# Layout of a gate scatter in PSUM, and which engine makes its operands and the lower parts of expert weights

## The chip, the cores and the metric

The kernel runs on one core of one Trainium2 chip. A core has TensorE (matrix products into PSUM), VectorE, ScalarE and GpSimd (element-wise work), SyncE (which issues most transfers) and 16 DMA engines. In the profile they are PE, DVE, ACT, POOL and SP, and PEld is the loading of weights into TensorE. The metric is device microseconds (us) of one execution, and less is better.

## The reference

Two layers act on 256 latent and 256 context tokens of width 1024. A layer is a modulated norm, one input projection, four token mixers, their gated merge, and then PEER, a retrieval from 16384 single-neuron experts laid out as a 128 by 128 grid. Only PEER matters here:

```python
def peer(x, wq, keys, u_tab, v_tab):
    q = (x @ wq).reshape(t, PEER_HEADS, 2, PEER_DK // 2)
    s = jnp.einsum('thpd,hpnd->thpn', q, keys)
    sv, si = lax.top_k(s, PEER_TOPK)                 # 16 best rows and 16 best columns of the grid
    cand = sv[:, :, 0, :, None] + sv[:, :, 1, None, :]
    best, pos = lax.top_k(cand, PEER_TOPK)           # 16 best experts per head, 8 heads
    eidx, g = ..., jax.nn.softmax(best, axis=-1)
    act = jax.nn.gelu(jnp.einsum('tkd,td->tk', u_tab[eidx], x))
    return jnp.einsum('tk,tkd->td', g * act, v_tab[eidx])
```

## The kernel before

The first layer routes 512 tokens and the last one 256. The experts of the first 128 tokens of layer 0 are gathered row by row; for all other tokens (three tiles of 128 in layer 0, two in the last layer) the kernel sweeps over all experts. For the sweep it needs, for every token, a dense 128 by 128 map of gates, G[i, j], which is zero but for the chosen experts.

**The scatter** (`scatter`, from line 1449) builds that map on TensorE: for one token, the product of one-hot rows (`ohA`, 128 slots by 128 rows i) and gated one-hot columns (`ohC`, 128 slots by 128 columns j). A tile is 32 steps `q` of four tokens. `hot` (L1468) makes `ohA` or `ohB` for eight tokens in one VectorE comparison, so there are 16 of each per tile. `gated` (L1482, L1484) multiplies four tokens of `ohB` by the gate `gT` and writes `ohC`: on ScalarE as four instructions, one for each token, or as one instruction on GpSimd or VectorE. The table `acts_of` and `pools_of` choose by `q % 5`: in layer 0 ScalarE has 2 and 4 and GpSimd 0, 1 and 3; in the last layer ScalarE has 4, GpSimd 0, 1 and 3, VectorE 2. A step then makes eight matmuls of 128 columns (L1505; a gate is two float16 parts, so two for each token). ScalarE copies the result out of PSUM (L1507) into `blk`, which holds 32 tokens and is stored to DRAM.

The matmuls write token after token, 128 values each. `blk` has the token innermost (32 of them), so that copy reads PSUM in order and writes single values 128 bytes apart.

**Beside the scatter** VectorE finds the best keys and experts of other tiles (`lists`, `select`; in `select` a loop over 15 ranks has one L1427 and one L1428 each), and TensorE computes the first products of the sweep for some expert tiles ahead of time (`u_mm`, L386 to L388: 24 matmuls for each expert tile, into `po`). Their weights come in as `wraw`; ScalarE rounds them to `wh` (L1210), and `wl = wraw - wh`, the lower part, is a subtraction on GpSimd or VectorE (L1211, chosen in `split_u`). Layer 0 computes up to 20 expert tiles ahead, the last layer up to 36.

What the order is set by: the code is written as generators that are interleaved by hand (`both`, `fill.step`), and a scheduler then sets the order of each engine's instructions. Buffers limit how far one engine runs ahead: five or six of `ohC`, three or four of `ohA`, three PSUM tiles `at`. Each engine takes its instructions in order.

Of the kernel before, what the change touches and what calls it, by code (L numbers as in the profile page):

```python
# [13 lines left out]
AF = mybir.ActivationFunctionType  # L14
# [5 lines left out]
P = 128  # L20
# [15 lines left out]
# column offsets in the constant block; the part from N_CST on is used for the Hyena filters only  # L36
# [10 lines left out]
# column offsets in the per-layer small block (partition layout); the part from N_SM on as above  # L47
# [4 lines left out]
# the per-layer row block, broadcast over the partitions  # L52
# [3 lines left out]
# pieces of the modulation: all, those of the first norm, and those that are not for the end of a layer only  # L56
# [4 lines left out]
# those that come during a layer's sweep; but for the first norm's, the last layer needs those of the latents only  # L61
# [3 lines left out]
def unit_order():  # L65
    """the order in which pieces of the weights are used: (layer, kind, index)"""
    o = []
    for l in range(DEPTH):
# [9 lines left out]
        # these are used for one half of the tokens after the other  # L78
# [62 lines left out]
def lay_out(i):  # L141
# [10 lines left out]
    def cols(w):  # L152
        """pieces of 128 columns: [partition = row of a block of 128 rows, block, column]"""
        m = w.shape[1] // 128
        return list(w.reshape(KD, P, m, 128).transpose(2, 1, 0, 3).reshape(m, P, 1024))

    def rows(w):
        """pieces of 4 blocks of rows by 256 columns"""
        m = w.shape[1] // 256
        return list(w.reshape(2, 4, P, m, 256).transpose(3, 0, 2, 1, 4).reshape(2 * m, P, 1024))  # L160
# [63 lines left out]
class Filler:  # L224
    """tensor-engine work that is emitted between the steps of latency-bound work"""
# [29 lines left out]
# of the gates, for their float16 parts  # L255
G_SCALE = 2.0 ** 15
# expert tiles whose first product may run ahead of the second, per layer: in buffers of their own, and in all
NE_OWN = (10, 20)
NE = (20, 36)
# the last expert tiles' second products go result by result  # L260
# [3 lines left out]
def body(ctx, tc, I, out, dbg=None):  # L264
# [28 lines left out]
    class Units:  # L293
# [41 lines left out]
        def next(self, kind):  # L335
            assert order[self.n][1] == kind, (order[self.n], kind)
            # stop at the end of a phase: what follows has other users of the buffers
# [42 lines left out]
    # ---------------------------------------------------------------- helpers  # L380
# [3 lines left out]
    def mm3(ps, w, x, first, last):  # L384
        """one k-step of an exact product of (hi, lo) pairs"""
# [4 lines left out]
    def rstd_of(dst, raw, inv, m):  # L390
        """dst = 1 / sqrt(inv raw + eps), the function's value refined by a Newton step; m is scratch"""
# [6 lines left out]
    def rstd_small(dst, raw, inv, m, t):  # L398
        """the same without the table of another function: a first value from the exponent's bits, three Newton steps"""
# [12 lines left out]
    def table_for_rstd():  # L412
        """loads the activation table that the next rstd_of needs, as soon as no other is needed before"""
# [6 lines left out]
    class Rms:  # L420
        """1/rms over the features of tokens t0..t1, the same on all partitions; fed chunk by chunk"""
# [7 lines left out]
        def square(self, k):  # L429
            if self.ring is None:  # L430
                self.sq[k] = self.sqp.tile([P, T], F32, name="n_sq", bufs=3)
            else:
                # in the memory of weights, which is free at this time
# [5 lines left out]
        def sum(self, k):  # L439
            """pairs of chunks are added first"""  # L440
# [16 lines left out]
    def norm_apply(rm, coef, ia, ib, tok=None):  # L457
        """modulated rows, split; tok takes those of the first 128 tokens with the tokens on the partitions"""
# [35 lines left out]
    def coef_of(l, u, s0=0):  # L494
        """coefficients of a norm, once the modulation is there up to unit u"""
# [7 lines left out]
    def adaln_row(l, u, w, crow, junk):  # L503
        """one piece of the modulation, its columns on the partitions, by the vector engine"""
# [7 lines left out]
    def adaln_lat(l, u, w, crow):  # L512
        """the same for the latents only"""
# [5 lines left out]
    # ---------------------------------------------------------------- start  # L519
# [15 lines left out]
    def adaln_first():  # L535
        """shift and scale of the first norm, two pieces of each at a time"""
# [27 lines left out]
    # ---------------------------------------------------------------- layers  # L564
    for l in range(DEPTH):
# [5 lines left out]
        with ExitStack() as ex:  # L571
# [4 lines left out]
            # the second layer's latents come first  # L576
# [1214 lines left out]
```

## Time and profile before

| | |
|---|---|
| timed runs, us | 3177.6, 3180.3, 3173.1; median 3177.6 |
| span of the profiled execution, us (of its time outside the span the profile shows nothing) | 3172.5 |
| PE, DVE, ACT, POOL busy, share of the span | 93%, 75%, 46%, 27% |

TensorE is busy nearly everywhere. The five tiles of the scatter are the longest stretches in which it is not. They are called A to E here and reach from the ScalarE copy that brings in a tile's rows `iT` to the next tile's, C and E to the last copy `g_first` of their layer: A 684.2 to 742.7, B 742.7 to 820.2, C 820.2 to 887.2 (layer 0), D 2373.4 to 2470.4, E 2470.4 to 2537.7 (last layer). C and E are the last tiles of their layers, which the code calls final. A row of the windows gives the length of a stretch and the time for which each engine was busy in it; where an engine is busy for nearly the whole length, the stretch can't be shorter than its work.

### The profile page before, as it was taken

Reading aid. Unit: us, or ns where it says so; the run is one execution under the profiler, and the core shown is the slowest. Engines: PE = TensorE matmul, PEld = TensorE weight load, DVE = VectorE, ACT = ScalarE, POOL = GpSimd, SP = SyncE. Lnnn points to the kernel's source line nnn. Section 1 sums busy time; section 2 is a strip of 40 time slices with the busy share of each in tenths; the row PEclk is TensorE's granted clock in tenths of the full one; section 3 lists DMA queues with packets and bytes.
Section 4 is the critical chain, followed back from the end, with each engine's and each line's share of the span. In section 5 each row is a group of like instructions: output and inputs, shape, how many; then the busy total and the mean of one; then the engine's idle time right before and its main releaser. Section 6 shows DMA issues by size and latency. Waiting matters only on the chain.

```text
span 3172.5 us, 47568 instructions
## 1 busy us (share of the span) xinstructions
PE 2946.5 (93%) x17500; PEld 2586.1 (82%) x17500; DVE 2387.9 (75%) x4801; ACT 1448.1 (46%) x2367; POOL 854.4 (27%) x557
## 2 busy tenths in 40 slices
PE   8999999977889999999999898999987799999998
PEld 6877778876778998888888796789877698889997
DVE  5775877799988777777878798758689877555555
ACT  5544423558843333323333234465447654555544
POOL 1001100355535454555555411000056300000000
PEclk9999999988889999999999999999989899999999
DMA  7232345434379888898888776334544498666663
GB/s 262 71 113 74 123 141 171 160 113 176 144 268 308 303 297 290 294 323 284 291 286 309 274 270 221 85 114 132 192 135 177 167 318 287 210 206 214 208 196 133
DMA packets 262506, 661.44 MB, mean 208 GB/s; under 512 B 21464, under 2 KB 113632, under 8 KB 261760
## 3 DMA queue, kind: packets, MB, share of 16 engines
q1 hardware_dynamic: 221808, 513.35, 48.3%
q0 software_dynamic: 40464, 145.05, 13.1%
q8 instruction: 137, 2.24, 0.3%
q14 instruction: 97, 0.79, 0.1%
HBM read 609.03 MB, written 49.29 MB: 208 GB/s over the span
## 4 chain that ended last, share of the span: by engine, by line
PE 39%; DVE 17%; issue 12%; DMA 11%; POOL 7%; ACT 2%; POOLq 0%; DVEq 0%; ACTq 0%; SPq 0%
PE mm L1637 6%; PE at L1637 6%; DMA grow<-in_V_dram,gix 6%; POOL grow L1273 5%; PE po L388 4%; PE po L386 4%; PE po L387 4%; PE mm L386 4%; PE mm L387 4%; PE mm L388 4%; POOL wl L1211 2%; DVE ohB L1468 2%; DMA grow<-in_UR_dram,gix 2%; DVE ohA L1468 1%; DMA wraw<-in_W_dram 1%
## 5 line engine op out<-in xcount | busy, mean ns | idle before, releaser
L388 PE MATMUL po<-nh,wl 128*128 128x384 f32 (+1 forms) x2048 | 649.3, 317 | 32.7 <-DVE wl L1211 28.3
L386 PE MATMUL po<-nh,wh 128*128 128x384 f32 (+1 forms) x2048 | 649.3, 317 | 13.7 <-ACT ga L1232 7.8
L387 PE MATMUL po<-nl,wh 128*128 128x384 f32 (+1 forms) x2048 | 645.8, 315 | 0.0
L1210 ACT ACTIVATE vh<-vr 128x1024 fp32r<-128x1024 f32 x254 | 269.5, 1061 | 617.6 <-DMA vr<-in_V_dram 493.1
L388 PEld LDWEIGHTS po<-nh,wl 128*128 128x128 f32 x2048 | 398.3, 194 | 40.8 <-DVE wl L1211 34.0
L386 PEld LDWEIGHTS po<-nh,wh 128*128 128x128 f32 x2048 | 398.0, 194 | 25.3 <-ACT ga L1232 9.3
L387 PEld LDWEIGHTS po<-nl,wh 128*128 128x128 f32 x2048 | 398.3, 195 | 7.4
L1211 DVE TENSOR_TENSOR vl<-vr,vh 128x1024 fp32r<-128x1024 f32 x254 | 334.3, 1316 | 84.7 <-ACT vh L1210 84.3
L1210 ACT ACTIVATE wh<-wraw 128x1024 fp32r<-128x1024 f32 x256 | 269.2, 1053 | 212.9 <-PE po L387 171.2
L386 PE MATMUL mm<-nh,wh 128*128 128x256 f32 (+1 forms) x1056 | 347.7, 331 | 10.0 <-ACT nh L482 3.9
L387 PE MATMUL mm<-nl,wh 128*128 128x256 f32 (+1 forms) x1056 | 342.9, 326 | 0.1
L388 PE MATMUL mm<-nh,wl 128*128 128x256 f32 (+1 forms) x1056 | 341.4, 324 | 0.4 <-POOL wl L326 0.4
L325 ACT ACTIVATE wh<-wraw 128x1024 fp32r<-128x1024 f32 x156 | 164.7, 1057 | 299.5 <-PE mm L387 194.8
L1211 DVE TENSOR_TENSOR wl<-wraw,wh 128x1024 fp32r<-128x1024 f32 x158 | 199.7, 1265 | 122.1 <-ACT wh L1210 122.0
L1211 POOL TENSOR_TENSOR wl<-wraw,wh 128x1024 fp32r<-128x1024 f32 x98 | 241.9, 2471 | 157.0 <-ACT wh L1210 155.6
L1637 PE MATMUL mm<-vl,Wh 128*128 128x512 f32 x635 | 251.8, 397 | 12.1 <-DVE vl L1211 11.7
L1637 PE MATMUL mm<-vh,Wh 128*128 128x512 f32 x635 | 249.6, 393 | 6.6 <-ACT vh L1210 6.5
L1637 PE MATMUL at<-vh,Wh 128*128 128x512 f32 x635 | 250.2, 394 | 0.0
L1637 PE MATMUL mm<-vh,Wl 128*128 128x512 f32 x635 | 249.5, 393 | 0.0
L1637 PE MATMUL at<-vh,Wl 128*128 128x512 f32 x635 | 249.3, 393 | 0.0
L1637 PE MATMUL at<-vl,Wh 128*128 128x512 f32 x635 | 249.2, 392 | 0.0
L1280 DVE SCALAR_TENSOR_TENSOR grow<-grow,mtok 128x1024 f32<-128x1024 f32 x128 | 167.2, 1321 | 106.4 <-DMA grow<-in_UR_dram,gix 106.3
(357 smaller groups left out, 6205.6 us busy)
## 6 DMA issues: line engine op xcount, KB each, us to landing
wraw<-in_U_dram SPq DMA_DIRECT2D x256, 512.0 KB
vr<-in_V_dram SPq DMA_DIRECT2D x254, 512.0 KB
wraw<-in_W_dram SPq DMA_DIRECT2D x190, 512.0 KB
gd<-gblk SPq DMA_DIRECT2D x80, 512.0 KB
G<-gd SPq DMA_DIRECT2D x32, 768.0 KB
grow<-in_W_dram SPq DMA_DIRECT2D x48, 512.0 KB
G<-gd SPq DMA_DIRECT2D x32, 512.0 KB
mw<-in_W_dram SPq DMA_DIRECT2D x16, 512.0 KB
```

The costliest lines, as they stand in the source:

```text
L325: act.activation(h, r, AF.Copy)
L386: pe.matmul(ps, w[0], x[0], start=first, stop=False)
L387: pe.matmul(ps, w[0], x[1], start=False, stop=False)
L388: pe.matmul(ps, w[1], x[0], start=False, stop=last)
L1210: act.activation(h, r, AF.Copy)
L1211: return eng.tensor_tensor(lo, r, h.bitcast(F32), op=ALU.subtract)
L1273: pool.indirect_dma_start(out=q[-1], out_offset=None, in_=tab, in_offset=bass.IndirectOffsetOnAxis(ap=gix[:, p, e:e + 1], axis=0))
L1280: dve.scalar_tensor_tensor(g, g, 1.0, mtok, op0=ALU.mult, op1=ALU.mult, accum_out=dot[:, e:e + 1])
L1468: dve.tensor_tensor(o, iota4[:, None].to_broadcast([P, 2, P, 4]), x[:, t:t + 8].rearrange("p (a b) -> p a b", b=4)[:, :, None, :].to_broad ...
L1637: pe.matmul(accs[i][h], w[a][:, i * 128:(i + 1) * 128], v[b][:, h * 512:(h + 1) * 512], start=j == 0 and a + b == 0, stop=j == P - 1 and a ...
```

## The change

Three edits, and the removal of the comments (three lines are added in all, so that lines behind them have numbers one to three higher):

```diff
-            acts_of = (((2, 4), (2, 4)), ((4,), (4,)))
-            pools_of = (((0, 1, 3), (0, 1, 3)), ((0, 1, 3), (0, 1, 3)))
+            acts_of = (0, 1, 2, 4), (2, 4)
...
-                acts, pools = [x[last][final] for x in (acts_of, pools_of)]
+                acts = acts_of[final]
...
-                        (pool if q % 5 in pools else dve).tensor_tensor(C, B.rearrange("p j t -> p t j"),
+                        dve.tensor_tensor(C, B.rearrange("p j t -> p t j"),
...
-                    ps = at_tile()
+                    ps4 = at_tile().rearrange("p (j t) -> p j t", t=4)
...
-                            pe.matmul(ps[:, z * 128:(z + 1) * 128], A[:, :, z], C[:, z, :, h], start=h == 1, stop=h == 0)
+                            pe.matmul(ps4[:, :, z], A[:, :, z], C[:, z, :, h], start=h == 1, stop=h == 0)
...
-                    evac[0] = act.activation(blk[:, :, o:o + 4].rearrange("p j t -> p t j"),
-                                   ps.rearrange("p (t j) -> p t j", j=128), AF.Copy, scale=1.0 / G_SCALE)
+                    evac[0] = act.activation(blk[:, :, o:o + 4], ps4, AF.Copy, scale=1.0 / G_SCALE)
...
-            halves(h, lo, ur.pop(j), pool if j < (own + 4 if last else 20) or (not last and j % 2) else dve)
+            halves(h, lo, ur.pop(j), lo_eng[0] or (pool if not last and j % 2 else dve))
...
+        lo_eng = [pool if last else dve]
...  in routing(), ahead of the first scatter:
+                lo_eng[0] = dve
...  behind routing() and fill.flush():
+            lo_eng[0] = None
```

1. The four tokens of a step lie innermost in PSUM: a matmul writes 128 values that are 16 bytes apart, and the copy reads PSUM in order and writes runs of four values (16 bytes), 128 bytes apart.
2. GpSimd makes no `ohC`. ScalarE makes 26 of the 32 of tiles A, B and D and 12 of C and E, VectorE the others: 104 or 48 instructions on ScalarE and 6 or 20 on VectorE.
3. `wl` moves by stage: on VectorE while a layer's scatter runs, on GpSimd before it in the last layer, and as before in the sweep.

On ScalarE at the start of tile A, this is the order before (`gblk` is the copy out of PSUM, with the shape that it writes; x4 are the four instructions of one `ohC`):

```order
L1459 ACTIVATE jT<-at 128x128
L1210 ACTIVATE wh<-wraw 128x1024
L1232 ACTIVATE ga<-po_7110 128x384
L1482 ACTIVATE ohC<-ohB,gT 128x128 x4
L1507 ACTIVATE gblk<-at 128x4x128
L1482 ACTIVATE ohC<-ohB,gT 128x128 x4
L1507 ACTIVATE gblk<-at 128x4x128
L1482 ACTIVATE ohC<-ohB,gT 128x128 x4
L1507 ACTIVATE gblk<-at 128x4x128 x2
L1482 ACTIVATE ohC<-ohB,gT 128x128 x4
L1507 ACTIVATE gblk<-at 128x4x128 x3
```

And this is the order on ScalarE at the same place now:

```order
L1460 ACTIVATE jT<-at 128x128
L1483 ACTIVATE ohC<-ohB,gT 128x128 x12
L1509 ACTIVATE gblk<-at 128x128x4 x3
L1483 ACTIVATE ohC<-ohB,gT 128x128 x16
L1509 ACTIVATE gblk<-at 128x128x4
L1483 ACTIVATE ohC<-ohB,gT 128x128 x4
L1509 ACTIVATE gblk<-at 128x128x4
L1483 ACTIVATE ohC<-ohB,gT 128x128 x4
L1509 ACTIVATE gblk<-at 128x128x4
L1483 ACTIVATE ohC<-ohB,gT 128x128 x4
```

ScalarE has about twice the `ohC` between two copies, and the shape of the copy has turned.

On VectorE at the start of tile E, after the gates `gT`, this is the order before:

```order
L1461 SCALAR_TENSOR_TENSOR gT<-at,gT 128x128
L1468 TENSOR_TENSOR ohB<-iota_21480,jT 128x1024
L1468 TENSOR_TENSOR ohA<-iota_21480,iT 128x1024
L1484 TENSOR_TENSOR ohC<-ohB,gT 128x512
L1468 TENSOR_TENSOR ohB<-iota_21480,jT 128x1024
L1468 TENSOR_TENSOR ohA<-iota_21480,iT 128x1024
L1468 TENSOR_TENSOR ohB<-iota_21480,jT 128x1024
L1468 TENSOR_TENSOR ohA<-iota_21480,iT 128x1024
L1484 TENSOR_TENSOR ohC<-ohB,gT 128x512
```

And this is the order on VectorE at the same place now:

```order
L1462 SCALAR_TENSOR_TENSOR gT<-at,gT 128x128
L1469 TENSOR_TENSOR ohB<-iota_21564,jT 128x1024
L1485 TENSOR_TENSOR ohC<-ohB,gT 128x512 x2
L1469 TENSOR_TENSOR ohA<-iota_21564,iT 128x1024
L1485 TENSOR_TENSOR ohC<-ohB,gT 128x512
L1469 TENSOR_TENSOR ohB<-iota_21564,jT 128x1024
L1469 TENSOR_TENSOR ohA<-iota_21564,iT 128x1024
L1485 TENSOR_TENSOR ohC<-ohB,gT 128x512
L1469 TENSOR_TENSOR ohB<-iota_21564,jT 128x1024
L1469 TENSOR_TENSOR ohA<-iota_21564,iT 128x1024
L1485 TENSOR_TENSOR ohC<-ohB,gT 128x512
L1211 TENSOR_TENSOR wl<-wraw,wh 128x1024
```

VectorE now makes more than half of the final tile's `ohC`, and lower parts stand between them. On GpSimd all 100 `ohC` are gone, and of 98 lower parts of `u_mm` 63 are left: 54 in layer 0's sweep, as before, and 9 ahead of tile D.

Counted in the order up to each tile's last instruction on the engine: the first products' matmuls on TensorE in A to E were 54, 192, 155, 337, 313 and are 68, 216, 153, 213, 432. The `wl` on VectorE in A to E were 0, 0, 1, 1, 4 and are 5, 7, 5, 11, 11.

## Rows read from the trace of the kernel before

**Rows 1.** The page: the span of the profiled execution.

```profile
span 3172.5 us, 47568 instructions
```

**Rows 2.** Windows of A to E: length, busy us (count) by engine, clock, DMA.

```profile
684.20:742.70 58.50, 44.45 (x352) 38.38 (x352) 56.49 (x152) 51.67 (x95) 27.83 (x22) 0.76 0.35 140
742.70:820.20 77.50, 60.36 (x452) 55.29 (x450) 74.73 (x214) 58.80 (x106) 46.70 (x29) 0.85 0.43 154
820.20:887.20 67.00, 53.79 (x432) 48.42 (x433) 64.23 (x219) 52.83 (x97) 36.14 (x24) 0.85 0.42 157
2373.40:2470.40 97.00, 71.09 (x622) 66.28 (x622) 95.63 (x272) 60.65 (x95) 58.27 (x33) 0.89 0.45 158
2470.40:2537.70 67.30, 54.48 (x522) 51.39 (x522) 52.57 (x52) 52.77 (x84) 28.08 (x20) 0.91 0.49 180
sum 367.30, PE 284.17 PEld 259.76 DVE 343.64 ACT 276.72 POOL 197.02; mean PE 56.83 PEld 51.95 DVE 68.73 ACT 55.34 POOL 39.40
```

**Rows 3.** Groups by line: busy us, mean ns, idle before and its releasers.

```profile
L1505 PE MATMUL at<-ohC,ohA 128*128 128x128 f16 x1280 | 107.8, 239 | 60.9 <-DVE ohA L1468 36.2 <-ACT gblk L1507 15.1 <-POOL ohC L1484 4.2
L1484 POOL TENSOR_TENSOR ohC<-ohB,gT 128x512 f32<-128x512 f16 x100 | 129.8, 1309 | 109.3 <-DVE ohB L1468 52.4 <-PE at L1505 32.6 <-DVE gT L1461 12.0
```

**Rows 4.** Timeline, VectorE then GpSimd: start us, duration us, engine, line, operation.

```profile
762.69 0.67 DVE L1468 TENSOR_TENSOR ohA<-iota,iT 128x1024 f16<-128x1024 f16 x1
763.28 0.08 DVE L1330 MATCH_VALUE_LOAD rep<-sv,mm 128x8 f32 x1
773.55 2.75 DVE L1468 TENSOR_TENSOR ohB<-iota,jT 128x1024 f16<-128x1024 f16 x1
772.90 2.85 POOL L1211 TENSOR_TENSOR wl<-wraw,wh 128x1024 fp32r<-128x1024 f32 x1
```

**Rows 5.** Windows of lines 1468 (in E, summed), 1428 and 1427 (summed).

```profile
2470.40:2537.70 67.30, 30.38 (x32) 0.91 0.49 180
sum 367.30, DVE 170.19; mean DVE 34.04
sum 367.30, DVE 27.40; mean DVE 5.48
sum 367.30, DVE 19.87; mean DVE 3.97
```

**Rows 6.** Single lines on VectorE: shortest/median/longest ns, first and last start.

```profile
L1428 DVE COPY_PREDICATED ij<-sf,sif x90: 421/446/2590, 669.4 to 2468.9; 128x256 f32<-128x256 uint16 x90
L1427 DVE TENSOR_SCALAR sf<-ab x90: 199/226/2340, 669.0 to 2468.6; 128x256 f16<-128x256 f16 x90
L1484 DVE TENSOR_TENSOR ohC<-ohB,gT x12: 678/1541/2758, 2380.1 to 2511.2; 128x512 f32<-128x512 f16 x12
L1211 DVE TENSOR_TENSOR wl<-wraw,wh x158: 1205/1225/3404, 874.2 to 3089.8; 128x1024 fp32r<-128x1024 f32 x158
```

**Rows 7.** ScalarE: two rows of the timeline, two groups by shape.

```profile
775.25 2.48 ACT L1482 ACTIVATE ohC<-ohB,gT 128x128 f32<-128x128 f16 x8
762.88 2.89 ACT L1507 ACTIVATE gblk<-at 128x512 f32<-128x512 f32 x3
L1507 ACT ACTIVATE gblk<-at 128x512 f32<-128x512 f32 x160 | 160.3, 1113 | 19.4 <-PE at L1505 18.7
L937 ACT ACTIVATE k<-at 128x512 f32<-128x512 f32 x48 | 28.6, 596 | 31.8 <-PE at L382 31.4 <-ACT wb L331 0.2
```

**Rows 8.** TensorE: four rows of the timeline; the windows of the keys.

```profile
775.51 0.67 PE L1505 MATMUL at<-ohC,ohA 128*128 128x128 f16 x8 [0.55 <-ACT gblk L1507]
775.98 0.42 PE L386 MATMUL po<-nh,wh 128*128 128x384 f32 x1
769.44 0.33 PE L388 MATMUL po<-nh,wl 128*128 128x384 f32 x1
769.61 0.33 PE L386 MATMUL po<-nh,wh 128*128 128x384 f32 x1
sum 367.30, PE 14.93 PEld 12.52 POOL 0.00; mean PE 2.99 PEld 2.50 POOL 0.00
```

More of the change, by code (lines that the diff above doesn't have):

```diff
@@ L1483, in gated @@
                     else:
-                        (pool if q % 5 in pools else dve).tensor_tensor(C, B.rearrange("p j t -> p t j"),
-                                                                    gT[:, t:t + 4][:, :, None].to_broadcast([P, 4, P]), op=ALU.mult)
+                        dve.tensor_tensor(C, B.rearrange("p j t -> p t j"),
+                                          gT[:, t:t + 4][:, :, None].to_broadcast([P, 4, P]), op=ALU.mult)
                     Cs[q] = C.rearrange("p t j -> p (t j)").bitcast(F16).rearrange("p (t j s) -> p t j s", t=4, s=2)
```

## Prediction

> **What bounds the kernel now.** I read the windows by slice first. TensorE is busy nearly everywhere, so only a stretch in which it idles or runs at the low clock can give time back, and the five tiles of the scatter, A to E, are the longest. They take 367.3 us of a span of 3172.5 [rows 1, 2]; TensorE is busy for 284.2 of that, so it idles 83, and its granted clock is 0.76 to 0.91, which means that part of the time it runs at the lower of its two levels (1.2 instead of 2.4 GHz). Then I looked for the engine without gaps: in A to D VectorE is busy 291.1 of 300.0 us (97%). In E no engine fills the stretch: TensorE has 54, VectorE and ScalarE 53 each of 67 [rows 2]. The groups by line confirm it: the scatter's matmuls wait longest for `ohA` from VectorE, then for the copy out of PSUM by ScalarE [rows 3]. So A to D are as long as VectorE's work there.
>
> Last I looked at single instructions on VectorE. The same one-hot takes 0.67 us, and the next instruction starts 0.59 after it, or 2.75 us; the slow one began while GpSimd was in a subtraction of 2.85 us, and both ended about together [rows 4]. Two-input work on VectorE and GpSimd holds each other up. The change takes GpSimd out of the scatter.
>
> **VectorE, part by part, in A to D.**
> One-hots: 170.2 us in all, 30.4 of them in E, so 139.8 for 128 in A to D [rows 5]. At 0.59 they are 76: **-64**.
> The loop over ranks in `select` (three passes of 15, all in A, B and D) takes 27.4 + 19.9 = 47.3 us; at its medians, 0.446 + 0.226, 45 pairs are 30 [rows 5, 6]: **-17**. Other two-input instructions of `select` gain too; I count nothing for them.
> `ohC`: 38 instead of 6. The shortest of before is 0.678, their median 1.54 [rows 6]. 38 at 0.68 less 6 at 1.54: **+17**. If they stayed at 1.54 with GpSimd idle, it would be +49; I take the shortest, because the long ones stood beside GpSimd.
> `wl`: 28 instead of 2 at 1.225 [rows 6]: **+32**. They had been hidden on GpSimd; now they stand in the queue ahead of the one-hots that TensorE waits for.
> Sum: 291 - 64 - 17 + 17 + 32 = 259. At the same 97% that is 267 us instead of 300, 11% less: B's 77.5 becomes 69, C's 67 becomes 60, D's 97 becomes 86.
>
> **ScalarE.** An `ohC` is four instructions, 0.31 each in a row (2.48 for eight), and a copy 0.96 (2.89 for three) [rows 7]. A, B and D get 14, 14 and 20 `ohC` more, 56, 56 and 80 instructions: +17, +17, +25 us. Against this stands the copy: written 128 bytes apart value by value it takes 1.113, while a copy of the same size that reads PSUM and writes in order takes 0.596 [rows 7]. No row shows runs of four values. The bounds are 0.596 and 1.113; I take 0.60, the nearer case in kind, since neighbours come together again. In proportion a copy then costs 0.52 in a row instead of 0.96, 14 us less per tile. ScalarE's work becomes about 55, 62, 38 and 71 in A to D, below or level with VectorE's. So ScalarE isn't the bound, but in B and D it is close, and it needs the cheaper copy for that.
> The Trainium skill (SBUF — State Buffer, Specifications (TRN2)) gives SBUF lines of 16 bytes and a penalty for each access that crosses to a new one. A run of four float32 is one such line, so by this rule the copy costs the contiguous 0.60; without it, 1.11, the third rival below.
>
> **TensorE.** Eight scatter matmuls take 0.47 (775.51 to 775.98), 59 ns each; a first product of 384 columns in layer 0 takes 0.17 (769.44 to 769.61), and one of 256 columns in the last layer by its columns 0.116 [rows 8]. With the counts of the new order a tile has 256 x 0.059 = 15 us of scatter, and first products of 68 x 0.174 = 12, 216: 38, 153: 27 (layer 0), 213 x 0.116 = 25 and 432: 50. The products with the keys, 15 us in all, go to A to D. So TensorE needs 31, 56, 46, 43 and 65 us at the full clock.
> To this comes what a matmul costs whose 128 results lie 16 bytes apart. The trace shows no such matmul. Lower bound: nothing. Upper bound: ScalarE's rate when it writes apart, 0.96 us for 512 values, 1.9 ns each, 243 ns for 128, so +185 ns per matmul. Between the two I take the ratio by which ScalarE's copy is slower apart than in order, 1.113 / 0.596 = 1.87: 110 instead of 59 ns, +52 ns, 13.3 us per tile. That makes 44, 69, 59, 56 and 78.
> In A, C and D this lies beside VectorE's 259; in B it is level with it. In E it decides: 78 instead of 67.3, also because 432 first products stand there instead of 313 and VectorE, which loses 11 us on one-hots, is not needed for so long.
>
> **Sum.** A to D 267 (-33), E 78 (+11): **-22 us**. First products that move between tiles, and lists that moved ahead, are inside these numbers. GpSimd's lower parts in layer 0 that ran ahead of A go to VectorE too, 3 us by the order, but the selection that stands there also stops meeting GpSimd; I count 0 for the two. The sweep behind, where TensorE is the bound and `wl` goes as before, is taken as unchanged. The profiled span of 3172.5 becomes 3150, and the median of the runs shown, 5 above that span, 3177.6 - 22 = **3155**. Late next is TensorE in E and B, and ScalarE in D.
>
> **The rivals.**
> *TensorE pays more for the stride* (slower). Place: the eight matmuls of every step; price up to +185 ns each. Then the tiles need on TensorE 31, 56, 46, 43, 65 with 47 us more each: 78, 103, 93, 90, 112, in all 476 instead of 367: **3287**. It decides from about +100 ns per matmul, where 241 + 1280 x 0.1 = 369: eight matmuls would then take 1.27 us instead of 0.47. For it: nothing else in the trace writes PSUM apart, and ScalarE shows that writing apart is not free; TensorE already has the longest work in E. Against it: TensorE idles 83 us there and runs partly at the low clock, so the first part of the price is covered.
> The Trainium skill (PSUM — Partial Sum Buffer, Specifications (TRN2)) speaks for this one: PSUM lines are 8 bytes, and any access pattern that isn't contiguous "slows matmuls significantly"; it gives no figure. By it the rival's chance can't be small, and a zero price is unlikely.
> *The stride costs TensorE nothing.* E falls to 65, A to D stay with VectorE: 332 instead of 367, -35, and the uncounted instructions of `select` may add 2 or 3: **3140**. For it: a matmul of 384 columns goes at the same rate per column as one of 128 [rows 8], so PSUM writing isn't seen to limit anything now.
> *The copy stays at 1.11* (the edit of the layout does nothing for ScalarE). Then ScalarE has 69, 76, 53 and 85 in A to D. It sets A and B, VectorE sets C (60) and D (86), and with E at 78 that is 369, no change: **3179**. For it: the runs are still 128 bytes apart. Against it: three of four values follow their neighbour.
>
> **Chances and range.** Moderate stride price as summed: 0.45. No price: 0.22. More than +100 ns: 0.21. Copy unchanged: 0.12. The first case by itself spans 3130 to 3175, because the share of 97% may drop when VectorE, ScalarE and TensorE come so near to each other. To hold 8 in 10 the range goes down to 3115 (no price, and more gain in `select`), and up to 3220 (+130 ns per matmul: 241 + 166 = 407 instead of 367, and a few us more). What a measurement of this kernel can tell from no change is about 0.2%, 6 us. Faster: 0.45 x 0.85 + 0.22 x 0.97 + 0.12 x 0.3 = 0.63; slower: 0.21 x 0.95 + 0.45 x 0.05 + 0.12 x 0.25 = 0.25; the same: the rest, 0.12.
>
> **What the profile would show.** Right: one-hots of 0.67 us nearly everywhere in the five tiles; copies near 0.60; eight scatter matmuls in 0.8 to 1.0 us; A to D together near 267 with VectorE busy over 94%; E longer than 67. Eight matmuls in 0.47 would be the second rival, in 1.3 or more the first; copies of 1.1 the third. The prediction falls altogether if one-hots stay slow without GpSimd, or if the time comes or goes outside the five tiles.

## The result, and where the time went

The kernel after takes 3129.9 us in the median (3123.5 to 3141.8, four runs); the kernel before, on the same chip, takes 3176.3 (3173.1 to 3180.3). The ratio is 0.987, 95% interval 0.984 to 0.989. In the profiled executions the span falls from 3172.5 to 3125.5, by 47.0 us. Lines 1468, 1484, 1505 and 1507 of before are 1469, 1485, 1507 and 1509 now.

The windows of the five tiles of after, bounded as in [rows 2]; the columns are length, busy us (count) of PE, PEld, DVE, ACT and POOL, TensorE's granted clock, DMA share and GB/s:

```profile
679.90:742.50 62.60, 52.42 (x359) 45.59 (x360) 57.00 (x221) 55.39 (x152) 0.00 (x0) 0.94 0.38 142
742.50:817.80 75.30, 72.25 (x494) 67.17 (x493) 69.44 (x285) 62.33 (x162) 0.00 (x0) 0.98 0.45 163
817.80:875.20 57.40, 53.29 (x386) 50.57 (x385) 54.34 (x162) 44.01 (x103) 2.39 (x1) 0.97 0.59 219
2338.40:2416.60 78.20, 66.04 (x497) 61.48 (x497) 72.26 (x275) 62.54 (x165) 0.00 (x0) 0.92 0.47 170
2416.60:2488.20 71.60, 71.60 (x618) 70.89 (x618) 51.20 (x70) 52.99 (x117) 0.00 (x0) 1.00 0.59 205
sum 345.10, PE 315.61 PEld 295.69 DVE 304.25 ACT 277.26 POOL 2.39; mean PE 63.12 PEld 59.14 DVE 60.85 ACT 55.45 POOL 0.48
```

Against [rows 2] A has grown by 4.1 us and E by 4.3; B, C and D are shorter by 2.2, 9.6 and 18.8. That is -22.2 in the tiles. GpSimd has left them (197.0 us busy, now 2.4), TensorE's work is done at a higher granted clock (A 0.94 instead of 0.76), and in E it is busy from end to end: 71.60 of 71.60.

The groups of after by line (busy us, mean ns, and idle time of the engine before them with what ended it); the matmuls and the copy answer to [rows 3, 7], the one-hots to [rows 5]:

```profile
L1507 PE MATMUL at<-ohC,ohA 128*128 128x128 f16 x1280 | 163.1, 313 | 15.8 <-ACT gblk L1509 13.1 <-DVE sf L1429 0.7 <-DVE ohC L1485 0.6
...
L1509 ACT ACTIVATE gblk<-at 128x512 f32<-128x512 f32 x160 | 92.6, 598 | 17.9 <-PE at L1507 17.4
...
L1469 DVE TENSOR_TENSOR ohA<-iota,iT 128x1024 f16<-128x1024 f16 x80 | 54.3, 681 | 10.2 <-PE at L1507 10.2
L1469 DVE TENSOR_TENSOR ohB<-iota,jT 128x1024 f16<-128x1024 f16 x80 | 54.3, 679 | 3.6 <-ACT ohC L1483 3.6
```

The one-hots take 0.68 us wherever they stand (shortest 0.662, longest 0.696). In before, the windows give 170.2 us for them, in after 105.8. A copy takes 0.598 instead of 1.113. TensorE's idle time before scatter matmuls is 15.8 us instead of 60.9, and what ends it is the copy.

TensorE in E (start, duration, line, operation). The sixteen scatter matmuls of two steps stand between first products, so the start of the next product shows where they end:

```profile
2443.40 0.28 PE L388 MATMUL po<-nh,wl 128*128 128x256 f32 x1
2443.52 1.94 PE L1507 MATMUL at<-ohC,ohA 128*128 128x128 f16 x16
2445.21 0.36 PE L386 MATMUL po<-nh,wh 128*128 128x256 f32 x1
2445.41 0.28 PE L387 MATMUL po<-nl,wh 128*128 128x256 f32 x1
```

Sixteen matmuls reach from 2443.52 to 2445.21, 106 ns each, where [rows 8] has 59. The granted clock is 1.00 in E now.

The other 24.8 us of the 47.0 lie outside the tiles: A starts 4.3 us earlier, between C's end and D's start there are 23.0 less (1486.2, now 1463.2), and behind E there are 2.5 more. Three pairs of rows tell of the middle part. First the indices that start layer 0's gather (the row-by-row fetch of the experts of the first 128 tokens), which `select` of tile 0 makes at its end (count, shortest/median/longest ns, first and last start), in before and in after:

```profile
L1438 DVE SCALAR_TENSOR_TENSOR gix<-ij x1: 282/282/282, 916.4 to 916.4; 128x128 int32<-128x128 f32 x1
```

```profile
L1440 DVE SCALAR_TENSOR_TENSOR gix<-ij x1: 282/282/282, 894.7 to 894.7; 128x128 int32<-128x128 f32 x1
```

They come 21.7 us earlier while C's end comes 12.0 earlier. Then the start of D, TensorE's transposition of D's `ij`, with the idle time before it and its releaser in brackets, in before and in after:

```profile
2372.49 0.90 PE L382 MATMUL at<-kc,ij 128*128 128x128 f32 x3 [10.19 <-DVE ij L1428]
```

```profile
2337.47 0.90 PE L382 MATMUL at<-kc,ij 128*128 128x128 f32 x3 [5.25 <-DVE ij L1430]
```

TensorE waits 4.9 us less there for the loop over ranks. Last comes the middle of layer 0's sweep, as a window from 1180 to 1780 in before and in after:

```profile
1180.00:1780.00 600.00, 570.09 (x2818) 513.31 (x2817) 468.27 (x466) 186.85 (x268) 318.92 (x206) 0.99 0.86 295
```

```profile
1180.00:1780.00 600.00, 572.78 (x2860) 516.47 (x2859) 473.88 (x464) 191.66 (x275) 327.51 (x208) 0.99 0.87 298
```

The code is the same there, yet TensorE executes 2860 instructions in these 600 us instead of 2818. Whether that belongs to the change is asked below.

### The profile page after: what moved, and what is told of

Its sections match the earlier page's. It is cut to its first block, busy times and chain, and to the rows that moved or that the text cites. A ratio compares the mean times of both kernels' runs of the same rounds, so it can differ in the third digit from the quotient of the medians.

```text
span 3125.5 us, 47587 instructions
## 1 busy us (share of the span) xinstructions
PE 2969.2 (95%) x17500; PEld 2615.0 (84%) x17500; DVE 2330.2 (75%) x4882; ACT 1447.3 (46%) x2583; POOL 640.8 (21%) x422
## 4 chain that ended last, share of the span: by engine, by line
PE 51%; DVE 12%; DMA 10%; issue 8%; POOL 5%; ACT 2%; POOLq 0%; DVEq 0%; ACTq 0%; SPq 0%
PE mm L1640 8%; PE at L1640 8%; PE po L388 6%; PE po L386 6%; PE po L387 6%; DMA grow<-in_V_dram,gix 5%; PE mm L386 4%; PE mm L387 4%; PE mm L388 4%; POOL grow L1275 3%; PE at L1507 2%; POOL wl L1211 2%; DMA vr<-in_V_dram 1%; DMA wraw<-in_W_dram 1%; DMA grow<-in_UR_dram,gix 1%
## 5 line engine op out<-in xcount | busy, mean ns | idle before, releaser
L387 PE MATMUL po<-nl,wh 128*128 128x384 f32 (+1 forms) x2048 | 639.0, 312 | 0.0
L1211 DVE TENSOR_TENSOR wl<-wraw,wh 128x1024 fp32r<-128x1024 f32 x193 | 239.7, 1243 | 128.6 <-ACT wh L1210 128.4
L386 PEld LDWEIGHTS mm<-nh,wh 128*128 128x128 f32 x1056 | 203.6, 194 | 35.4 <-issue 6.0
```

The costliest lines, as they stand in the source:

```text
L386: pe.matmul(ps, w[0], x[0], start=first, stop=False)
L387: pe.matmul(ps, w[0], x[1], start=False, stop=False)
L1211: return eng.tensor_tensor(lo, r, h.bitcast(F32), op=ALU.subtract)
```

## The experiments

All times are medians, and ratios are to the kernel before with a 95% interval. In the table tiles are bounded by TensorE alone, so that all kernels are measured alike: from the first transposition of a tile's `ij` to that of the next, C and E to the last scatter matmul. The stretches come from one profiled execution of each kernel, the last column is the median of all. `gix` to D reaches from the indices to D's start, and "rows" from the issue of the first fetched row of layer 0's gather to that of the last. By these bounds before has 364.2 us in the tiles and after 343.8.

| kernel | A | B | C | D | E | sum | C's end to D | `gix` to D | rows | us |
|---|---|---|---|---|---|---|---|---|---|---|
| before | 55.7 | 80.3 | 65.7 | 97.0 | 65.5 | 364.2 | 1487.5 | 1456 | 882 | 3176 |
| after | 58.4 | 77.8 | 57.7 | 77.8 | 72.1 | 343.8 | 1464.6 | 1443 | 876 | 3130 |
| e1 layout undone | 63.3 | 82.6 | 61.4 | 87.4 | 66.4 | 361.2 | 1476.4 | 1453 | 884 | 3159 |
| e2 turned by the copy | 56.2 | 72.4 | 56.6 | 77.1 | 60.4 | 322.6 | 1480.9 | 1457 | 890 | 3125 |
| e3 pairs | 58.3 | 76.2 | 57.7 | 78.7 | 72.0 | 342.9 | 1468.2 | 1446 | 881 | 3129 |
| e4 GpSimd in vain | 69.4 | 83.9 | 73.0 | 87.2 | 87.1 | 400.7 | 1475.1 | 1453 | 886 | 3189 |
| e5 lower parts undone | 56.8 | 72.4 | 60.0 | 76.4 | 81.5 | 347.0 | 1487.5 | 1471 | 899 | 3154 |
| e6 columns back | 74.8 | 65.9 | 61.9 | 90.6 | 65.6 | 358.6 | 1473.2 | 1458 | 889 | 3155 |
| e7 layout alone | 55.8 | 79.1 | 68.0 | 96.9 | 67.2 | 367.0 | 1491.1 | 1461 | 890 | 3173 |
| e8 lists late | 56.9 | 79.5 | 63.6 | 75.6 | 72.6 | 348.1 | 1492.4 | 1440 | 874 | 3155 |
| e9 after again | 58.5 | 76.2 | 56.3 | 78.6 | 72.1 | 341.6 | 1472.7 | 1451 | 886 | 3134 |
| e10 turned, balanced | 54.7 | 76.0 | 57.1 | 76.6 | 68.9 | 333.4 | 1468.1 | 1453 | 885 | 3127 |
| e11 four rows | 57.1 | 81.4 | 55.7 | 78.5 | 72.0 | 344.8 | 1407.6 | 1383 | 818 | 3070 |
| e12 e10 and e11 | 55.4 | 77.8 | 57.3 | 75.9 | 70.2 | 336.6 | 1408.2 | 1395 | 829 | 3061 |

**e1: the layout undone.**

```diff
-                    ps4 = at_tile().rearrange("p (j t) -> p j t", t=4)
+                    ps = at_tile()
-                            pe.matmul(ps4[:, :, z], ...
+                            pe.matmul(ps[:, z * 128:(z + 1) * 128], ...
-                    evac[0] = act.activation(blk[:, :, o:o + 4], ps4, ...
+                    evac[0] = act.activation(blk[:, :, o:o + 4].rearrange("p j t -> p t j"), ps.rearrange("p (t j) -> p t j", j=128), ...
```

> The kernel after, with PSUM laid out token by token again (matmuls write in order, the copy writes apart); engines and lower parts as after. Theory: the layout was needed because ScalarE got the columns. Copies go from 0.60 back to 1.11 us, +14 us of ScalarE per tile: 69, 76, 58 and 77 us of work in A to D where after has stretches of 62.6, 75.3, 57.4 and 78.2, so A to D grow by about 20; matmuls fall from 106 to 59 ns, and E loses 2 to 4. Sum about +18: 3148, 0.991 of before. Rival: ScalarE has room for the old copy, and the stride only costs TensorE time: A to D unchanged, E from 71.6 to 60: 3118 to 3120.

3158.6 us, 0.994 (0.9915 to 0.9963). The groups of its matmuls and its copy:

```profile
L1507 PE MATMUL at<-ohC,ohA 128*128 128x128 f16 x1280 | 121.1, 249 | 58.1 <-ACT gblk L1509 46.8 <-DVE ohA L1469 3.3 <-DVE ohC L1485 1.9
L1509 ACT ACTIVATE gblk<-at 128x512 f32<-128x512 f32 x160 | 164.8, 1107 | 3.3 <-PE at L1507 3.1
```

The copy takes 1.107 us again, and TensorE waits 46.8 us for it. A to D grow by 23, E falls by 5.7: together 17.4, as the theory has it. The whole is 10 us above the forecast, because another 12 lie between C's end and D's start. The rival falls: with the columns on ScalarE, the kernel needs the cheaper copy.

**e2: the copy turns.** PSUM as in e1, and the copy reads apart what it writes in runs:

```diff
+                    evac[0] = act.activation(blk[:, :, o:o + 4], ps.rearrange("p (t j) -> p j t", j=128), ...
```

> The kernel after, with PSUM laid out token by token (matmuls write in order), and the copy itself turns: it reads PSUM 512 bytes apart and writes runs of four values. Theory: the old copy's price, 1.11 instead of 0.60 us, is that of writing value by value to places 128 bytes apart; reading PSUM apart costs little. Copies 0.60 to 0.65, matmuls 59 ns: E, bound by TensorE at 71.6, falls to 62 to 64 (ScalarE and VectorE have 53 and 51), A to D stay or lose 5: 3115 to 3122, 0.982 of before. Rival: ScalarE pays for walking apart on either side: copies 1.0 to 1.1, and the time is that of the layout undone, about 3148.

3124.9 us, 0.983 (0.980 to 0.986). That is 3 us above the forecast, and the difference from after is within the intervals. The groups, and sixteen scatter matmuls in E with the first product behind them:

```profile
L1507 PE MATMUL at<-ohC,ohA 128*128 128x128 f16 x1280 | 112.5, 242 | 28.7 <-ACT gblk L1509 25.1 <-DVE ohC L1485 1.7 <-DVE sf L1429 1.0
L1509 ACT ACTIVATE gblk<-at 128x512 f32<-128x512 f32 x160 | 90.0, 600 | 8.6 <-PE at L1507 8.1
...
2441.76 1.13 PE L1507 MATMUL at<-ohC,ohA 128*128 128x128 f16 x16
2442.70 0.36 PE L386 MATMUL po<-nh,wh 128*128 128x256 f32 x1
```

The copy takes 0.600 us though it reads PSUM 512 bytes apart, and a matmul takes 59 ns again (16 in 0.94 us). So the price of 1.113 in before lay on the side that writes single values, and TensorE need not pay for the layout. E falls from 72.1 to 60.4 and the tiles by 21. Of this only about 5 us arrive in the whole: D starts 7 us later than in after, though C ends 9 earlier. The table shows where the rest goes: from `gix` to D's start it takes 1457 us instead of 1443, and that is the gather, 890 us from the first row to the last instead of 876. In A and D TensorE's granted clock is 0.71 and 0.77, where after has 0.92 in both: with the shorter matmuls TensorE stands idle for longer there (26.9 us of the two stretches, in after 20.5).

**e3: pairs.** Two tokens innermost in PSUM:

```diff
+                    ps2 = at_tile().rearrange("p (a j t) -> p a j t", a=2, t=2)
+                            pe.matmul(ps2[:, z // 2, :, z % 2], A[:, :, z], ...
+                    evac[0] = act.activation(blk[:, :, o:o + 4].rearrange("p j (a t) -> p j a t", t=2), ps2.rearrange("p a j t -> p j a t"), ...
```

> The kernel after, with two tokens innermost in PSUM instead of four: a matmul's results lie 8 bytes apart instead of 16, the copy reads pairs and still writes runs of four. Theory: a matmul pays because each value falls into a line of its own; at 8 bytes this holds as at 16, so matmuls stay at 106 ns and the time at 3130 (E 71.6). Rival: the price grows with the distance: 59 ns at 4 bytes, 106 at 16, so 75 at 8, E falls by 6 to 66: 3123. Copies 0.60 if reading in pairs is free; at 1.1 A to D grow by 20.

3128.8 us, 0.985 (0.982 to 0.989). Scatter matmuls in E and the first product behind them:

```profile
2442.63 1.94 PE L1507 MATMUL at<-ohC,ohA 128*128 128x128 f16 x16
2444.33 0.36 PE L386 MATMUL po<-nh,wh 128*128 128x256 f32 x1
```

Sixteen in 1.70 us, 106 ns each: results 8 bytes apart cost what they cost 16 bytes apart, and the rival falls. The Trainium skill (PSUM — Partial Sum Buffer, Specifications (TRN2)) has lines of 8 bytes and says that matmuls are slowed significantly by an access that isn't contiguous; the 106 ns of TensorE's writing agree with it. In e2 ScalarE's reading shows no such price.

**e4: GpSimd in vain.** After, and for three of five steps

```diff
+                        X = gp.tile([P, 4, P], F16, name="ohX", bufs=1)
+                        pool.tensor_tensor(X, iota4.rearrange("p j t -> p t j"), gT[:, t:t + 4]..., op=ALU.mult)
```

> The kernel after, and beside it GpSimd multiplies a constant table by the gates for three of five steps, as it did for the columns before, into a tile that nobody reads (written as float16). Nobody waits for it. Theory: two-input work on GpSimd holds up that on VectorE, whatever waits for it: the one-hots go from 0.66 to a mean of 0.9 to 1.1 us, A to E grow by 35 to 60 us: 3165 to 3190. Rival: before lost its time because VectorE and TensorE queued behind results that GpSimd delivered late: one-hots stay at 0.66 to 0.70, and the time at 3130, within 5.

3189.3 us, 1.004 (1.002 to 1.006): slower than before. One-hots, and GpSimd's instruction:

```profile
L1469 DVE TENSOR_TENSOR ohA<-iota,iT 128x1024 f16<-128x1024 f16 x80 | 75.9, 952 | 2.9 <-PE at L1511 2.8
L1469 DVE TENSOR_TENSOR ohB<-iota,jT 128x1024 f16<-128x1024 f16 x80 | 74.3, 930 | 1.1 <-ACT ohC L1483 1.1
...
L1489 POOL TENSOR_TENSOR ohX<-iota,gT 128x512 f16<-128x512 f16 x100 | 140.0, 1400 | 213.0 <-DVE gT L1462 205.6
```

Nobody waits for `ohX`, yet the one-hots take 0.94 instead of 0.68 us and the tiles 400.7 instead of 343.8. VectorE is busy 373 us in them instead of 303. The queue behind late results, the rival, explains nothing of this: it is the two engines side by side. VectorE's work grows by half a microsecond for each that GpSimd works. The Trainium skill (SBUF — State Buffer, Who interferes with whom) says that a VectorE instruction with two inputs in SBUF contends with a GpSimd instruction that reads SBUF, for a port pair that is locked and not shared; the one-hots' 0.94 us fit that.

**e5: lower parts undone.**

```diff
-            halves(h, lo, ur.pop(j), lo_eng[0] or (pool if not last and j % 2 else dve))
+            halves(h, lo, ur.pop(j), pool if j < (own + 4 if last else 20) or (not last and j % 2) else dve)
```

> The kernel after, with the choice of the engine for the lower parts (wl) as in before: GpSimd while the scatter runs, layout and columns as after. Theory: GpSimd's two-input work costs VectorE about as much as it saves. From the run with GpSimd in vain: 142 us of GpSimd lengthened VectorE's work by 70, half a microsecond for each. 28 lower parts of 2.6 us are 73 us of GpSimd, so +36 on VectorE, and 28 x 1.2 = 34 go from it: A to E within 10 of after's 344, and 3130 to 3145 in all, since TensorE waits longer for each lower part. Rival: the move of the lower parts was a cost that the rest of the change paid for: VectorE loses 34 us of work in A to D, which is its bound, and the time falls to about 3105.

3153.9 us, 0.994 (0.991 to 0.997). In the tiles the theory holds, 347.0 us and so within 10 of 344: those of layer 0 are 4.7 us shorter than in after, E is 9.4 longer. But the whole costs more than the theory's upper end, because from `gix` to D's start it takes 28 more. The rival falls. Of the 28, 23 lie between the first and the last row of the gather, 899 us, the longest of all; what makes it the longest, I couldn't show.

**e6: the columns back on GpSimd.**

```diff
-            acts_of = (0, 1, 2, 4), (2, 4)
+            acts_of, pools_of = ((2, 4), (4,))[last], (0, 1, 3)
-                        dve.tensor_tensor(C, ...
+                        (pool if q % 5 in pools else dve).tensor_tensor(C, ...
```

> The kernel after, with the columns (ohC) divided as in before: GpSimd does steps 0, 1 and 3 of five; layout and lower parts as after. Theory: 100 columns of 1.3 us on GpSimd lengthen VectorE's work by 65 us and take 40 us of columns from it: +25, and E, where no VectorE time is to spare once its one-hots slow down, grows too. A to E about 365 instead of 344, 3145 to 3160. Rival: with the lower parts off GpSimd and the cheaper copies, the columns are no harm there, and VectorE and ScalarE have less to do: 3120 or lower.

3154.7 us, 0.995 (0.993 to 0.997), as the theory has it. The tiles take 358.6, and the scatter matmuls wait for one-hots again, 20.6 us:

```profile
L1507 PE MATMUL at<-ohC,ohA 128*128 128x128 f16 x1280 | 159.9, 318 | 27.2 <-DVE ohA L1469 20.6 <-POOL ohC L1485 3.4 <-ACT gblk L1509 2.9
```

**e7: the layout alone**, on the kernel before; three lines of the change:

```diff
+                    ps4 = at_tile().rearrange("p (j t) -> p j t", t=4)
+                            pe.matmul(ps4[:, :, z], ...
+                    evac[0] = act.activation(blk[:, :, o:o + 4], ps4, ...
```

> The kernel before with the new layout in PSUM alone: matmuls at 106 instead of 59 ns, copies at 0.60 instead of 1.11 us, engines as in before. Theory: in A to D VectorE held up by GpSimd sets the end, so the copies bring nothing or little there; in E TensorE gets 12 us more: 0 to +10, 3176 to 3186. Rival: the copy was a bound in itself (TensorE waited 15 us for it): 3155 to 3165, and the layout would be half of what the change brings.

3172.6 us, 1.000 (0.9991 to 1.0013); the profiled execution, at 3182.6, is the longest of ten. The copy falls to 0.592 us, the matmuls rise to 106 ns, and the tiles stay (367.0 by 364.2). In A to D VectorE is busy for 286.0 of 299.8 us, so both are hidden there, and E grows by 1.7. By itself this edit is worth nothing, and the rival falls.

**e8: lists late.**

```diff
-                    next(others, 0)
+                    if z >= 10:
+                        next(others, 0)
```

> The kernel after, with the lists of tile 0 begun in step 10 instead of step 0 of tile C: VectorE does the same work, but more of it behind C's last column. Theory: what starts layer 0's sweep is the end of VectorE's work (scatter and selection of tile 0 together), not the end of the scatter: C ends some 5 to 10 us earlier, the selection ends at the same time within 3 (its last index at 895), and the whole stays at 3130 within 5. Rival: the sweep follows C's end, so what C gains the whole gains: 3120 to 3125.

First products have by then overwritten the queries that these lists read, so tile 0's selection has other values here, in the same amount, and other rows are fetched. 3154.6 us, 0.995 (0.993 to 0.997). Both theories missed. C doesn't end earlier, and the selection ends 33 us later than in after:

```profile
L1440 DVE SCALAR_TENSOR_TENSOR gix<-ij x1: 278/278/278, 927.5 to 927.5; 128x128 int32<-128x128 f32 x1
```

The order has moved more than I meant: the lists had stood in B, where VectorE has gaps now (61 busy of 79.5 us), and stand behind C. What it shows is a link: `gix` 33 us later, C's end 2 later, the gather's last row 31 later (1801.9 instead of 1770.9), D's start 30 later. The sweep's second products begin at 893.1, as in after (891.7). So D doesn't follow the end of the scatter or the beginning of the sweep, but the gather, which starts at the end of the selection.

**e9: after again**, unchanged.

> The kernel after once more, unchanged. Between C's end and D's start its profile has 23 us less than before, and part of it lies in the middle of layer 0's sweep, which the change doesn't touch: from 1180 to 1780 us TensorE executes 2860 instructions in after, 2818 in before, and 2773 to 2817 in the eight other kernels. Theory: this is the spread of an execution. The new profile has 2780 to 2830 there, and C's end to D's start takes 1470 to 1485 instead of 1464.6; the median stays within 0.987 +- 0.002 of before. Rival: it belongs to the program: 2850 to 2870 and 1462 to 1468 again.

3134.3 us, 0.9875 (0.986 to 0.989).

```profile
1180.00:1780.00 600.00, 567.37 (x2806) 511.03 (x2805) 469.84 (x453) 188.27 (x269) 320.36 (x206) 0.98 0.86 293
```

2806 instead of 2860, and C's end to D takes 1472.7, as the theory has it. The window of 600 us is not a property of the change, and two profiles of one kernel differ by 8 us between C and D. Most of the 23 stays all the same. In both profiles `gix` comes 21.8 us after C's end where before has 31.4, and D starts 564 to 567 us after the gather's last row where before has 574: some 17 us in all. Between them lies the gather, with 876 and 886 us around before's 882.

**e10: turned, balanced.** On e2:

```diff
-            acts_of = (0, 1, 2, 4), (2, 4)
+            acts_of = ((0, 1, 2, 4), (0, 1, 2, 3, 4))[last], ((0, 2, 4), (2, 4))[last]
```

> The kernel in which the copy turns, and the columns divided anew: ScalarE makes all of D's (four of five before) and three of five of C's (two before). Theory: C and D are bound by VectorE (55 of 56.6 and 73 of 77.1 us, ScalarE 44 and 61); six columns of 0.68 less in each are -4 each, ScalarE then has 52 and 69: 3117 instead of 3125, 0.981 of before. Rival: other waits end last there by now, or the gain of the tiles is lost in the sweep behind: 3125.

3126.6 us, 0.985 (0.983 to 0.986). The rival holds: C has 57.1, D 76.6, as in e2. The five tiles are even 11 us longer than in e2, by B and E above all; but C's end to D is 13 shorter, of which 9 because `gix` comes 15 us after C's end instead of 24, and the whole is the same. VectorE has 66 of D's 76.6 us now, so it isn't the bound there any more. TensorE's longest wait in D is the one for copies, 15.5 us (10.9 in e2):

```profile
PE at L1507 <- ACT gblk L1509: 15.5, 17, 2.6
```

Whether this wait or the granted clock, 0.73 there, now sets D's end, no run separates.

**e11: four rows.** On after; in layer 0 the gathered rows have four buffers, and a row is fetched three ahead (and what makes room for it):

```diff
-            rows = lambda: up.tile([P, D], F32, name="grow", bufs=3)
+            rows = lambda: up.tile([P, D], F32, name="grow", bufs=4 - l)
-                for e in range(P + 2):
+                for e in range(P + 3):
...
-                    if e < 2:
+                    if e < 3:
                         continue
-                    e -= 2
+                    e -= 3
```

> The kernel after with four buffers instead of three for the gathered rows of layer 0, so that a row is fetched three ahead instead of two (to make room, four ohC instead of five in layer 0 and a lead of 4 instead of 5 steps; a junk tile in float16). Theory: in the sweep of layer 0 VectorE waits 125 us in the 600 between 1180 and 1780 for gathered rows; these waits stand ahead of wl and vl, for which TensorE then waits 27 us, and this sets how fast the sweep goes and why its time differs from kernel to kernel. One row more ahead: VectorE waits under 60, TensorE's idle time there falls by 15 to 25 us, and the whole to 3095 to 3115. Rival: rows come as fast as DMA brings them (its share is 0.87): the waits stay above 110, and so do 3130.

3069.8 us, 0.968 (0.9665 to 0.969): 60 us below after, where 15 to 35 were expected. VectorE's longest waits in the window from 1180 to 1780 (us in total, times, longest), in before and in after:

```profile
DVE gacc L1284 <- DMA grow<-in_V_dram,gix: 78.2, 35, 4.5
DVE grow L1280 <- DMA grow<-in_UR_dram,gix: 47.0, 26, 3.7
DVE gacc L1282 <- DMA grow<-in_V_dram,gix: 4.8, 1, 4.8
```

```profile
DVE gacc L1286 <- DMA grow<-in_V_dram,gix: 80.8, 38, 4.3
DVE grow L1282 <- DMA grow<-in_UR_dram,gix: 36.9, 19, 4.2
DVE gacc L1284 <- DMA grow<-in_V_dram,gix: 7.1, 1, 7.1
```

And in e11, with its window:

```profile
DVE grow L1282 <- DMA grow<-in_UR_dram,gix: 8.2, 6, 2.5
DVE gacc L1286 <- DMA grow<-in_V_dram,gix: 4.5, 4, 2.2
```

```profile
1180.00:1780.00 600.00, 599.93 (x3043) 547.69 (x3042) 510.62 (x519) 214.84 (x291) 322.75 (x202) 1.00 0.90 312
```

The waits for gathered rows fall from 125 us to 13, TensorE has no gap left, and it executes 3043 instructions instead of 2860. A row lands 6.1 to 6.7 us after its issue, by the median of the transfers in after:

```profile
grow<-in_UR_dram,gix POOLq DMA_INDIRECT x128, 6.7
grow<-in_V_dram,gix POOLq DMA_INDIRECT x128, 6.1
```

An expert tile is 42 matmuls (24 of the first product, 18 of the second), so 2860 are 68 tiles, 8.8 us each, and each uses two or three rows. With three buffers a row can't be fetched before the row three ahead of it has been used, and VectorE stands still until it lands, with `wl` and `vl` behind it in its queue. So the gather set the pace of layer 0's sweep in before, which has the same waits (130 us), and in after, and TensorE, 95% busy there, only looked like the bound.

The buffers are not all of it. In after, GpSimd and VectorE around one such wait:

```profile
1415.16 2.41 POOL L1211 TENSOR_TENSOR wl<-wraw,wh 128x1024 fp32r<-128x1024 f32 x1
1417.72 1.09 POOL L1275 DMA_INDIRECT grow<-in_V_dram,gix  x1 [0.16 <-issue]
1411.73 2.60 DVE L1286 SCALAR_TENSOR_TENSOR gacc<-grow,gdot,gacc 128x1024 f32<-128x1024 f32 x2
1425.94 1.28 DVE L1286 SCALAR_TENSOR_TENSOR gacc<-grow,gdot,gacc 128x1024 f32<-128x1024 f32 x1 [4.30 <-DMA grow<-in_V_dram,gix]
```

The buffer was free at 1414.3, but GpSimd, which issues the fetch, was in a lower part until 1417.6, so the fetch left 3.4 us late. Of the 58 waits for rows in this window, 26 follow a fetch that was held up like this, and they make up 68 of the 125 us. In e11 these fetches are as late, and VectorE no longer waits for them. Whether moving those lower parts off GpSimd would do as much as a fourth row, no run shows.

**e12: e10 and e11 together.**

> Both together: the copy turns, the columns are divided anew, and four rows are fetched ahead. If the parts add: 13 less than after from the scatter and 15 to 35 from the sweep: 3085 to 3105, 0.975 of before. If the gathered rows are bound by DMA: 3115 to 3125.

3061.1 us, 0.965 (0.964 to 0.966): better than both kernels, by 3.5% and 2.2%, and below the forecast, as e11 is. The parts add: e10 is 3 to 8 us below after and its repetition, e11 60 to 65, and e12 is 9 below e11.

## Why the prediction was right, and where it was not

It said 3155, faster; it is 3130, and the range of the forecast, 3115 to 3220, holds it. But the whole fell by 46 us where 22 were forecast. The sum over the five tiles was right to the digit, -22 by -22.2, and that is partly luck: A to D fell by 26.5 instead of 33, E grew by 4.3 instead of 11, and the two misses cancel.

- *One-hots, -64 in A to D.* They fall from 139.8 to 84.9 us, -55. The cause is right, and e4 shows it. The size was off because the 139.8 count each by its own time, which overlaps the next instruction, and the 0.59 count it to the start of the next. By either count on both sides it is -55 (to the start of the next, 132.2 and 77.1).
- *Rank loop -17:* 19.9 + 9.8 = 29.7 us instead of 47.3. Right.
- *`ohC` on VectorE, 38 at 0.68:* 27.0 us in A to D, where before has 11.3. *`wl`, 28 at 1.225:* 31 stand there, 34.2 us. Right.
- *VectorE in A to D, 259 us at 97%, so 267.* It is busy 253.0, which is 38 less than before where the sum has 32: the other instructions of `lists` and `select`, counted at nothing, gave 6 to 12, by the way of counting. But A to D take 273.5, so the share is 92%. The share was the weak step: with VectorE, ScalarE and TensorE so near to each other the tiles no longer go by one of them. In A VectorE has 57.0 of 62.6, and TensorE waits 6.0 us for copies.
- *Copy 0.60:* 0.598; by e2 and e1 it is the runs of four on the writing side that do it. The Trainium skill (SBUF — State Buffer, Specifications (TRN2)) has lines of 16 bytes and a penalty for each cross to a new line; the 0.598 for runs of 16 bytes and the 1.107 for single values agree.
- *Matmuls 110 ns:* 106. The ratio of ScalarE's copy was a lucky guide, but both rivals on the stride, none and over 100 ns more, fall.
- *E 78, TensorE-bound:* TensorE-bound it is, at 71.6. The term of the first products was too large: 360 start in the stretch, not 432. The others ran ahead of it, among the 129 first products that stand behind D's last scatter matmul, still in D's stretch.
- *GpSimd's lower parts and the selection ahead of A counted at 0:* A starts 4.3 us earlier, and the wait ahead of D is 4.9 shorter.
- *"The sweep behind … is taken as unchanged":* this step failed, and with it the criterion that the time comes from the five tiles alone: 24.8 of the 47.0 us, over half, came from outside. I had read 95% busy as TensorE being the bound. The pace of layer 0's sweep is set by the gathered rows (e11), and the gather starts at the end of tile 0's selection on VectorE (e8), which the change brings forward by 21.7 us. From `gix` to D's start the twelve profiles with three rows need 1440 to 1471 us, whatever the tiles do. C's end to D varies as much (1465 to 1492), so only e8, which moves the two far apart, tells which of them counts. In all fourteen profiles D starts 564 to 574 us after the gather's last row, so most of the spread, into which e2's gain fell, lies in the gather itself: 874 to 899 us with three rows. Two profiles of the same kernel differ there by 10; the rest is open.

Of the rivals, *the copy stays at 1.11* is nearest to e1, which has the matmuls at 59 ns besides: I gave it 3179, it is 3159.

The parts of the change need each other. Undoing the layout, the lower parts or the columns costs 29, 24 and 25 us, together more than the 46, and the layout alone brings nothing: it frees ScalarE for the columns that GpSimd no longer makes. The lower parts and the columns were not run alone. Of the lower parts' 24 us only 3 lie in the tiles and most of the rest in the gather; why it follows there is open.

## What to carry to other kernels

An engine that is 95% busy need not be the bound. Look at what ends its gaps, and what that engine waits for in turn (here `wl` and `vl` on VectorE, and behind them the gathered rows), and add one buffer to that chain before taking a stretch as fixed. Ask of a gain which later start it brings forward (here the gather's indices), because a stretch behind with its own pace can swallow it. And when a layout has to be turned, let the side turn it that pays nothing for it: try the read before the write.

## What the runs showed of the hardware

- A scatter matmul of 128 float16 columns takes 59 ns when its results lie in order, and 106 when they lie 8 or 16 bytes apart (e2, e3, after, all in E at a granted clock of 1.00).
- ScalarE copies 512 values per partition out of PSUM in 0.60 us, in order or 512 bytes apart, if it writes runs of 16 bytes, and in 1.11 if it writes single values 128 bytes apart (after, e2, e1).
- 140 us of GpSimd work that nobody waits for made VectorE's work in the tiles 70 us longer and the kernel 55 to 59 us slower (e4).
- A fetch of rows that GpSimd issues left 3.4 us after its buffer was free when GpSimd was in a subtraction of 2.41 us (after).
